# The up projection of a gated MLP: seven products of halves replaced by eight plain products

## The chip, the cores and the metric

The kernel runs on one core of a Trainium2 chip. The metric is the device time of one execution in microseconds (us). Engines are named as the profile names them: PE is TensorE (PEld its weight loads), DVE is VectorE, ACT is ScalarE, POOL is GpSimd, and SP is SyncE, whose queue issues nearly all DMAs here.

## The reference

Two layers of a block for a latent generator: a token mixer (a chunked state-space scan in both directions beside a diagonal recurrence) and a feed-forward part, for 1024 latent tokens and 256 context tokens of 1024 channels. The change concerns the feed-forward part only:

```python
def conv_ffn(h, w_up, conv_w, conv_b, w_down, rows):
    up = h @ w_up                                  # (tokens, 1024) x (1024, 2 * 2816)
    ...
    up = dwconv_centred(up, conv_w, conv_b)        # width 3 along tokens, within a grid row of 64
    gate, val = jnp.split(up, 2, axis=-1)
    return (jax.nn.silu(gate) * val) @ w_down      # (tokens, 2816) x (2816, 1024)
```

Layer 0 computes it for all 1280 tokens, layer 1 (the last) for the 1024 latent tokens alone. All data are float32.

## The kernel before

Activations lie with channels on the 128 partitions and tokens along the free dimension. A float32 operand is used as two parts, a rounded one (`hi`) and the remainder (`lo`), and each product is the sum of three matmuls, hi x hi, hi x lo and lo x hi (`mm3`, L746). Making the parts of an operand takes a cast on ACT and a subtraction on DVE or POOL (`split_act`, L977, for activations; `split_to`, L876, for weights).

The feed-forward part goes over the tokens in two blocks, called passes here: 640 tokens each in layer 0, 512 each in layer 1. In a pass (`ffn_halves`, L1492) the 2816 hidden channels are 22 tiles j, in 8 groups of 2 or 3. For the tiles of a group (and the first of the next one) `up(j)` computes 128 gate and 128 value channels into the two rows `fr0` and `fr1`; then `gate` applies the convolution (ACT L1511, DVE L1518 and L1520), SiLU and the product, and splits the result (`g`). Then the down products of the group are added to eight accumulators (`acc`, DVE L1597), with down weights that are loaded (`raw`, L1555) and split (`wd`, L880, L881) on the way. PSUM has four banks for these products (`psm`, tile `mm`).

The up products are done by a scheme of seven products instead of eight. The weights of tile j are four blocks (gate or value, first or second half of the 1024 input channels), the activations four blocks (first or second half of the input channels, first or second half of the block's tokens). `halves` (L844) makes the seven combinations of the activations, `lefts` (L884) those of the weights: three sums and one difference on POOL, seven splits by ACT with DVE (four) or POOL (three). Each of the seven operands is stored to DRAM (`kept`, L926), 512 KB each, and in the second pass it is loaded from there in place of the raw weights (L945). `seven` (L949) multiplies each with one half of the tokens, 4 x 3 matmuls of 320 columns (layer 0) or 256 (layer 1), and adds the results into `fr0` and `fr1` by DVE out of PSUM (L958).

The operands wait in a ring of slots (`ws`; 5 in layer 0, 7 in layer 1). `W.fill` fills it ahead of a tile, and after each product `W.step` makes the next one; the raw weights (`rw`) have 4 or 6 buffers. All instructions of an engine run in the order in which they are written; SP's loads and stores too. Between the products, `self.tick()` lets background work go on: the modulation vectors (`adaw`, only in layer 0's passes) and the streamed residual and norm of the other block (`stream`, L1621, tiles `xs`, `xk`), which load and store through SP's queue. `tail` makes the activations of the second pass during the last group's down products of the first.

## Time and profile before

| what | value |
|---|---|
| median of 3 runs | 3623.93 us (3618.96 to 3641.98) |
| profiled execution, its own time | 3592.94 us |
| its span, first to last instruction | 3591.1 us |
| mean granted clock of TensorE, share of full speed | 0.915 |
| PE busy | 3036.1 us, 85% |
| DVE busy | 2510.9 us, 70% |
| ACT busy | 1363.1 us, 38% |
| POOL busy | 1070.4 us, 30% |
| read from and written to DRAM | 471.33 MB, 271.09 MB |

The shares are means over the whole span, which has phases with different limits; the feed-forward passes run from 893 to 2011 us (layer 0) and from 2717 to 3577 us (layer 1). A busy PE counts from a matmul's start to its modelled end, so that neighbours overlap; the distance between starts tells what a matmul costs.

### The profile page before, as it was taken

Reading aid. Unit: us, or ns where it says so; the run is one execution under the profiler, and the core shown is the slowest. Engines: PE = TensorE matmul, PEld = TensorE weight load, DVE = VectorE, ACT = ScalarE, POOL = GpSimd, SP = SyncE. Lnnn points to the kernel's source line nnn. Section 1 sums busy time; section 2 is a strip of 40 time slices with the busy share of each in tenths; the row PEclk is TensorE's granted clock in tenths of the full one; section 3 lists DMA queues with packets and bytes.
Section 4 is the critical chain, followed back from the end, with each engine's and each line's share of the span. In section 5 each row is a group of like instructions: output and inputs, shape, how many; then the busy total and the mean of one; then the engine's idle time right before and its main releaser. Section 6 shows DMA issues by size and latency. Waiting matters only on the chain.

```text
span 3591.1 us, 53144 instructions
## 1 busy us (share of the span) xinstructions
PE 3036.1 (85%) x19123; PEld 2687.2 (75%) x19123; DVE 2510.9 (70%) x4661; ACT 1363.1 (38%) x2422; POOL 1070.4 (30%) x819
## 2 busy tenths in 40 slices
PE   7689869898688989889999789748887688889998
PEld 4578657687568989868899788746676677778997
DVE  5867963557757787855465897973578788876666
ACT  4324514545333333432122444514445444433223
POOL 3642441233324454200000332441245355510000
PEclk9899988898799999999999899878898899999999
DMA  7354587333886666787666445467256787768774
GB/s 244 107 159 149 156 242 218 114 108 112 273 289 215 222 233 217 262 307 247 230 226 215 132 122 168 129 186 200 91 161 218 271 282 264 270 251 295 265 281 180
DMA packets 583083, 745.94 MB, mean 208 GB/s; under 512 B 66116, under 2 KB 423118, under 8 KB 582821
## 3 DMA queue, kind: packets, MB, share of 16 engines
q1 hardware_dynamic: 582341, 742.38, 62.5%
q8 instruction: 152, 2.49, 0.3%
q14 instruction: 110, 0.90, 0.1%
q0 software_dynamic: 480, 0.17, 0.1%
HBM read 471.33 MB, written 271.09 MB: 207 GB/s over the span
## 4 chain that ended last, share of the span: by engine, by line
PE 37%; DVE 21%; DMA 6%; issue 4%; ACT 3%; SPq 1%; POOL 1%; DVEq 0%; ACTq 0%; POOLq 0%
PE mm L751 11%; PE mm L753 10%; PE mm L752 10%; PE ps L55 5%; DVE fc L1518 2%; DVE fc L1520 2%; DVE fr L958 2%; DVE ws L881 1%; DMA adaw<-in_w_ada_dram 1%; DVE X L550 1%; DVE sc L545 1%; ACT fc L1511 1%; DVE X L517 1%; DVE acc L1597 1%; DMA up<-ws 1%
## 5 line engine op out<-in xcount | busy, mean ns | idle before, releaser
L751 PE MATMUL mm<-unit,ws 128*128 128x320 f32 (+1 forms) x2464 | 749.2, 304 | 75.5 <-DVE fr L958 43.3
L753 PE MATMUL mm<-unit,ws 128*128 128x320 f32 (+1 forms) x2464 | 742.0, 301 | 6.5 <-DVE ws L881 4.3
L752 PE MATMUL mm<-unit,ws 128*128 128x320 f32 (+1 forms) x2464 | 742.6, 301 | 1.7 <-POOL unit L860 1.2
L751 PEld LDWEIGHTS mm<-unit,ws 128*128 128x128 f32 x2464 | 477.1, 194 | 103.7 <-DVE fr L958 49.1
L753 PEld LDWEIGHTS mm<-unit,ws 128*128 128x128 f32 x2464 | 477.7, 194 | 10.9 <-DVE ws L881 6.3
L752 PEld LDWEIGHTS mm<-unit,ws 128*128 128x128 f32 x2464 | 478.2, 194 | 6.5 <-issue 3.4
L958 DVE TENSOR_TENSOR fr<-mm,fr 128x320 f32<-128x320 f32 (+1 forms) x616 | 270.3, 451 | 277.7 <-PE mm L753 275.3
L751 PE MATMUL mm<-unit,whi 128*128 128x320 f32 (+3 forms) x1264 | 425.7, 338 | 38.3 <-ACT unit L979 23.4
L753 PE MATMUL mm<-unit,wlo 128*128 128x320 f32 (+3 forms) x1264 | 416.3, 330 | 9.7 <-POOL wlo L742 9.5
L752 PE MATMUL mm<-unit,whi 128*128 128x320 f32 (+3 forms) x1264 | 417.9, 331 | 7.0 <-POOL unit L980 5.6
L742 POOL TENSOR_TENSOR wlo<-raw,whi 128x1024 fp32r<-128x1024 f32 (+1 forms) x86 | 201.4, 2342 | 365.0 <-ACT whi L741 343.6
L751 PE MATMUL mm<-g,wd 128*128 128x320 f32 (+3 forms) x708 | 254.7, 361 | 60.5 <-ACT wd L880 36.2
L751 PEld LDWEIGHTS mm<-unit,whi 128*128 128x128 f32 x1264 | 250.4, 199 | 73.5 <-ACT unit L979 26.3
L1511 ACT ACTIVATE fc<-fr,fcols 128x640 f32<-128x640 f32 (+1 forms) x176 | 144.1, 862 | 350.4 <-DVE fr L958 350.2
L753 PE MATMUL mm<-g,wd 128*128 128x320 f32 (+3 forms) x708 | 249.6, 357 | 25.7 <-DVE wd L881 25.5
L1597 DVE TENSOR_TENSOR acc<-mm,acc 128x320 f32<-128x320 f32 (+3 forms) x336 | 183.2, 552 | 123.2 <-PE mm L753 122.4
L753 PEld LDWEIGHTS mm<-unit,wlo 128*128 128x128 f32 x1264 | 250.0, 198 | 24.9 <-POOL wlo L742 13.9
L752 PEld LDWEIGHTS mm<-unit,whi 128*128 128x128 f32 x1264 | 250.7, 198 | 19.7 <-POOL unit L980 6.5
L752 PE MATMUL mm<-g,wd 128*128 128x320 f32 (+3 forms) x708 | 251.4, 355 | 1.1 <-DVE g L1530 1.1
L1518 DVE SCALAR_TENSOR_TENSOR fc<-fr,fcols,fc 128x255 f32<-128x255 f32 (+2 forms) x220 | 190.5, 894 | 58.7 <-ACT fc L1511 57.5
L751 PEld LDWEIGHTS mm<-g,wd 128*128 128x128 f32 x708 | 142.0, 201 | 89.1 <-ACT wd L880 44.3
L881 POOL TENSOR_TENSOR ws<-rw,ws 128x512 fp32r<-128x512 f32 x88 | 133.2, 1515 | 219.4 <-ACT ws L880 214.6
(412 smaller groups left out, 6519.6 us busy)
## 6 DMA issues: line engine op xcount, KB each, us to landing
up<-ws SPq DMA_DIRECT2D x308, 512.0 KB
ws<-up SPq DMA_DIRECT2D x308, 512.0 KB
rw<-in_ffn_w_up_dram SPq DMA_DIRECT2D x176, 256.0 KB
adaw<-in_w_ada_dram SPq DMA_DIRECT2D x80, 512.0 KB
raw<-in_ffn_w_down_dram SPq DMA_DIRECT2D x96, 384.0 KB
raw<-in_w_in_dram SPq DMA_DIRECT2D x40, 512.0 KB
raw<-in_w_out_dram SPq DMA_DIRECT2D x32, 512.0 KB
unit<-in_w_ada_dram SPq DMA_DIRECT2D x32, 256.0 KB
```

Of the source, the lines that this page charges most:

```text
L55: i = f(*a, **k)
L517: v.scalar_tensor_tensor(o, col(g, a, k, nj), T["lam"][:, 0, i, g:g + 1], o, op0=OP.mult, op1=OP.add)
L742: (eng or nc.vector).tensor_tensor(lo[:, :m], raw[:, :m], hi[:, :m].bitcast(F32), op=OP.subtract)
L751: mm(ps, whi[:, k], ahi[:, sl], start=first and k == 0, stop=False)
L752: mm(ps, whi[:, k], alo[:, sl], start=False, stop=False)
L753: i = mm(ps, wlo[:, k], ahi[:, sl], start=False, stop=last and k == len(a) - 1)
L881: eng.tensor_tensor(lo, x, hi.bitcast(F32), op=OP.subtract)
L958: add = lambda o, ps, x: v.tensor_tensor(o, ps, x, op=OP.add)
L1511: nc.scalar.activation(c, r[s], AF.Identity, bias=f[3][:, ft:ft + 1], scale=f[1][:, ft:ft + 1])
L1518: v.scalar_tensor_tensor(cr[:, :, 1:], rr[:, :, :w - 1], f[0][:, ft:ft + 1], cr[:, :, 1:], op0=OP.mult, op1=OP.add)
L1520: v.scalar_tensor_tensor(cr[:, :, :w - 1], rr[:, :, 1:], f[2][:, ft:ft + 1], cr[:, :, :w - 1], op0=OP.mult, op1=OP.add)
L1597: v.tensor_tensor(acc[m][:, o:o + c], ps, acc[m][:, o:o + c], op=OP.add)
```

## The change

The up projection is computed as plain products. `splits` (in place of `halves`) splits each of the eight activation tiles, DVE and POOL in turn. `lefts` loads the raw weights of tile j in four pieces of 128 x 512, gate before value, splits each (ACT with POOL), stores nothing, and is given the list of all tiles twice, so that the second pass loads and splits the weights again. `ups` (in place of `seven`) multiplies a piece with all tokens of the block: four channel tiles x 3 matmuls for each piece of tokens (256 and 384, or 320 twice, in layer 0; 512 in layer 1). The first half of the channels opens the sum in PSUM and the second half closes it, and ACT copies the sum to `fr0` or `fr1`. A tile has four steps in place of seven; the gate of the tile before is advanced twice per step and background work after every second.

```diff
-    def halves(self, src, n, out, pool):
...
+    def splits(self, src, n, out, pool):
+        for k in range(KT):
+            out.append(self.split_act(src(k), n, self.nc.gpsimd if k % 2 else self.nc.vector))
             yield
...
-    def lefts(self, srcs, out, pool, kept):
...
+    def lefts(self, srcs, out, pool):
+        nc, g = self.nc, self.nc.gpsimd
+        todo = [(p, i) for p in srcs for i in range(2)]
+        raws = []
         def load():
             if todo:
                 p, i = todo.pop(0)
...
+                x = pool.tile([P, 4, P], F32, name="rw", bufs=self.nrw)
+                self.sp.last = nc.sync.dma_start(x, p[:, 4 * i:4 * i + 4])
+                raws.append(x)
+        for _ in range(3):
+            load()
         yield
...
+        while raws:
+            w = self.slot(pool)
+            out.append(self.split_to((w[:, 0], w[:, 1]), raws.pop(0), g))
+            load()
+            yield
+
+    def ups(self, W, b, n, pieces, r):
+        for t in r:
+            ps = [self.psm.tile([P, 512], F32, name="mm")[:, :c] for _, c in pieces]
+            for h in range(2):
+                w = W.take()
+                for (o, c), x in zip(pieces, ps):
+                    self.mm3(x, w, b[4 * h:4 * h + 4], slice(o, o + c), h == 0, h == 1)
+                if h:
+                    for (o, c), x in zip(pieces, ps):
+                        self.nc.scalar.copy(t[:, o:o + c], x)
                 yield
-    def seven(self, W, b, n, ra, rb):
...
-            for i, _ in enumerate(self.seven(W, B, n, *r)):
+            for i, _ in enumerate(self.ups(W, B, n, pieces, r)):
+                next(post, None)
                 next(post, None)
                 W.step()
-                if i in (2, 5):
+                if i % 2:
                     self.tick()
...
-        kept = [self.dram.tile([P, 7, 2, 4 * P], F32, name=f"up{l}{j}") for j in range(nt)]
-        LW = Stream(self.lefts([up(j) for j in range(nt)], ops, pw, kept), ops)
+        LW = Stream(self.lefts([x for _ in range(2) for j in range(nt) for x in up(j)], ops, pw), ops)
```

The calls of `halves` and `ffn_halves` become calls of `splits` and `ffn`, and `Stream.fill` stops when the generator is at its end.

## Rows read from the trace of the kernel before

**Rows 1.** Four passes: length, busy PE, PEld, DVE, ACT, POOL, clock, DMA share, GB/s.

```profile
893.00:1491.00 598.00, 498.07 (x3000) 460.52 (x2999) 451.72 (x731) 229.27 (x392) 247.23 (x175) 0.92 0.68 238
1491.00:2011.00 520.00, 489.92 (x3127) 449.94 (x3125) 306.60 (x622) 143.74 (x241) 26.85 (x23) 0.97 0.72 244
2717.00:3199.00 482.00, 382.95 (x2378) 340.24 (x2378) 390.66 (x566) 206.16 (x373) 229.88 (x156) 0.90 0.76 265
3199.00:3577.00 378.00, 364.90 (x2497) 333.49 (x2498) 246.43 (x490) 120.12 (x215) 2.02 (x2) 0.99 0.73 261
```

**Rows 2.** Timeline of TensorE, start and duration in us: 320, 256 and 512 columns.

```profile
1299.92 0.31 PE L751 MATMUL mm<-unit,ws 128*128 128x320 f32 x1
...
1303.89 0.31 PE L751 MATMUL mm<-unit,ws 128*128 128x320 f32 x1
...
3319.94 0.28 PE L751 MATMUL mm<-unit,ws 128*128 128x256 f32 x1
...
3322.76 0.28 PE L751 MATMUL mm<-unit,ws 128*128 128x256 f32 x1
...
3345.06 0.39 PE L751 MATMUL mm<-g,unit 128*128 128x512 f32 x1
...
3346.45 0.40 PE L751 MATMUL mm<-g,wd 128*128 128x512 f32 x1
```

**Rows 3.** Sums over up-product stretches: layer 0 first, second pass; layer 1 first, second.

```profile
sum 359.70, PE 309.96 PEld 290.94 DVE 273.35 ACT 150.07 POOL 167.13; mean PE 38.74 PEld 36.37 DVE 34.17 ACT 18.76 POOL 20.89
...
sum 308.50, PE 296.66 PEld 279.31 DVE 163.39 ACT 72.49 POOL 0.48; mean PE 37.08 PEld 34.91 DVE 20.42 ACT 9.06 POOL 0.06
...
sum 277.70, PE 241.68 PEld 236.58 DVE 236.81 ACT 127.88 POOL 156.59; mean PE 30.21 PEld 29.57 DVE 29.60 ACT 15.98 POOL 19.57
...
sum 222.80, PE 220.95 PEld 219.74 DVE 131.03 ACT 53.64 POOL 0.00; mean PE 27.62 PEld 27.47 DVE 16.38 ACT 6.71 POOL 0.00
```

**Rows 4.** Sums over down-product stretches, the same four passes in the same order.

```profile
sum 237.20, PE 185.57 PEld 168.31 DVE 179.78 ACT 81.34 POOL 81.73; mean PE 23.20 PEld 21.04 DVE 22.47 ACT 10.17 POOL 10.22
...
sum 203.60, PE 186.86 PEld 167.03 DVE 138.84 ACT 69.70 POOL 24.26; mean PE 23.36 PEld 20.88 DVE 17.35 ACT 8.71 POOL 3.03
...
sum 205.90, PE 142.50 PEld 104.68 DVE 155.44 ACT 80.13 POOL 74.35; mean PE 17.81 PEld 13.08 DVE 19.43 ACT 10.02 POOL 9.29
...
sum 141.90, PE 132.38 PEld 103.94 DVE 104.02 ACT 60.55 POOL 0.00; mean PE 16.55 PEld 12.99 DVE 13.00 ACT 7.57 POOL 0.00
```

**Rows 5.** Waits of TensorE, us, times, longest: layer 1 first, layer 0 second pass.

```profile
PE mm L751 <- ACT wd L880: 33.0, 6, 14.5
PE mm L751 <- DVE fr L958: 25.1, 17, 2.8
PE mm L753 <- DVE wd L881: 17.9, 9, 3.7
...
PE mm L751 <- ACT unit L859: 3.5, 1, 3.5
...
PE mm L751 <- DMA ws<-up: 8.1, 3, 3.6
```

**Rows 6.** Groups of GpSimd and ScalarE, first pass of layer 1: splitting an up weight.

```profile
L881 POOL TENSOR_TENSOR ws<-rw,ws 128x512 fp32r<-128x512 f32 x42 | 62.6, 1491 | 69.4 <-ACT ws L880 66.6 <-issue 2.8
...
L880 ACT CAST ws<-rw 128x512 fp32r<-128x512 f32 x84 | 50.6, 616 | 17.3 <-PE mm L753 13.0 <-POOL rw L923 2.8 <-DMA rw<-in_ffn_w_up_dram 1.1
```

**Rows 7.** Waits of SP's queue, first pass of layer 1.

```profile
SPq L55 <- POOL ws L881: 40.9, 24, 5.9
```

**Rows 8.** Groups of VectorE in layer 1: first pass, then (last row) second pass.

```profile
L958 DVE TENSOR_TENSOR fr<-mm,fr 128x256 f32<-128x256 f32 x154 | 61.9, 413 | 14.8 <-PE mm L753 14.1
L1518 DVE SCALAR_TENSOR_TENSOR fc<-fr,fcols,fc 128x504 f32<-128x504 f32 x44 | 54.7, 1262 | 16.7 <-ACT fc L1511 16.7
...
L1518 DVE SCALAR_TENSOR_TENSOR fc<-fr,fcols,fc 128x504 f32<-128x504 f32 x44 | 32.0, 743 | 20.3 <-ACT fc L1511 20.3
```

**Rows 9.** Busy time in one down stretch, second pass of layer 1.

```profile
3341.60:3358.40 16.80, 16.80 (x74) 13.52 (x74) 12.21 (x21) 6.27 (x12) 0.00 (x0) 1.00 0.46 166
```

More of the change, by code (lines that the diff above doesn't have):

```diff
@@ L88, in step @@
     def step(self):
-        next(self.gen, None)
+        return next(self.gen, self) is not self
     def fill(self, n):
-        while len(self.out) < n:
-            self.step()
+        while len(self.out) < n and self.step():
+            pass
     def take(self):
@@ L882, in split_to @@
         return hi, lo
-    def lefts(self, srcs, out, pool, kept):
-        nc, v, g = self.nc, self.nc.vector, self.nc.gpsimd
-        m = 4 * P
-        todo = [(p, i) for p in srcs for i in (2, 3, 0, 1)]
-        spots = iter([(d, i) for d in kept for i in range(7)])
-        late = []
-        def store():
-            w, (d, i) = late.pop(0)
-            self.sp.dma_start(d[:, i], w)
-        def put(x, eng):
-            w = self.slot(pool)
-            out.append(self.split_to((w[:, 0], w[:, 1]), x.rearrange("p (k n) -> p k n", n=P), eng))
-            late.append((w.bitcast(F32), next(spots)))
-            if len(late) > 2:
-                store()
+    def lefts(self, srcs, out, pool):
+        nc, g = self.nc, self.nc.gpsimd
+        todo = [(p, i) for p in srcs for i in range(2)]
+        raws = []
         def load():
@@ L940, in lefts @@
-        while late:
-            store()
-        for d in kept:
-            for i in range(7):
-                w = self.slot(pool)
-                self.sp.last = nc.sync.dma_start(w.bitcast(F32), d[:, i])
-                out.append([w[:, j].rearrange("p (k n) -> p k n", n=P) for j in range(2)])
-                yield
-    def seven(self, W, b, n, ra, rb):
-        v = self.nc.vector
-        lo, hi = slice(0, n // 2), slice(n // 2, n)
-        def mul(i):
-            ps = self.psm.tile([P, 512], F32, name="mm")[:, :n // 2]
-            self.mm3(ps, W.take(), b[i], slice(0, n // 2))
-            return ps
-        add = lambda o, ps, x: v.tensor_tensor(o, ps, x, op=OP.add)
-        self.nc.scalar.copy(ra[:, lo], mul(0))
-        yield
-        add(ra[:, hi], mul(1), ra[:, lo])
-        yield
-        add(rb[:, hi], mul(2), ra[:, hi])
-        yield
-        add(rb[:, lo], mul(3), rb[:, hi])
-        yield
-        ps = mul(4)
-        add(rb[:, hi], ps, rb[:, hi])
-        add(ra[:, hi], ps, ra[:, hi])
-        yield
-        add(ra[:, lo], mul(5), ra[:, lo])
-        yield
-        add(ra[:, hi], mul(6), ra[:, hi])
-        yield
+                x = pool.tile([P, 4, P], F32, name="rw", bufs=self.nrw)
@@ L1489, in wout, with ffn @@
         self.free(*itertools.chain(*a))
-    def ffn_halves(self, l, blk, B, W, new, pr, pool, pw, ng, before, tail, done):
+    def ffn(self, l, blk, B, W, new, pr, pool, pw, ng, before, tail, done):
         nc, v = self.nc, self.nc.vector
@@ L1570, in ffn_halves @@
             if gi + 1 == ng:
-                self.free(*itertools.chain(*itertools.chain(*B)))
+                self.free(*itertools.chain(*B))
                 for _ in post:
@@ L1618, in chain @@
         self.free(R)
-        yield from self.halves(lambda k: self.normed(mt, k, blk, S, A, B, pool), blk[1], out, pool)
+        yield from self.splits(lambda k: self.normed(mt, k, blk, S, A, B, pool), blk[1], out, pool)
     def stream(self, blk, md, R, G, A, B, hd, pool):
@@ L2054, in finish @@
             yield from self.prenorm(acc, blk, R[1], self.prs[1]["A1"], self.prs[1]["ada"], H[1], pn)
-        tail = self.halves(load(0), n1, H2[1], pn)
-        self.ffn_halves(l, blks[0], H2[0], LW, new, pr, pg, pw, 8, before, tail, away(md[1]))
+        tail = self.splits(load(0), n1, H2[1], pn)
+        self.ffn(l, blks[0], H2[0], LW, new, pr, pg, pw, 8, before, tail, away(md[1]))
         if last:
@@ L2063, in layer @@
             tail, done = first_next(), squares
-        acc = self.ffn_halves(l, blks[1], H2[1], LW, new, pr, pg, pw, 8, before, tail, done)
+        acc = self.ffn(l, blks[1], H2[1], LW, new, pr, pg, pw, 8, before, tail, done)
         if not last:
```

50 lines of the change are left out of this document (removed).

## The prediction

> **What bounds the kernel now.** I read the page's shares first, then the busy time of each engine in the four passes of the feed-forward part (two blocks of tokens in each of two layers), because the change touches nothing else. These passes last 598, 520, 482 and 378 us [rows 1], 1978 of the 3591 us span. The reader should compare the two passes of one layer: they do the same products, and yet the first is 78 us longer than the second in layer 0 and 104 us longer in layer 1. In the second passes TensorE is busy nearly throughout at a granted clock of 0.97 and 0.99 (the upper level, 2.4 GHz, but for a few moments); in the first it is busy 83% and 79% of the time, at 0.92 and 0.90, which mixes in stretches at the lower level after waits. The first passes differ in one thing: there the weights are loaded, combined by GpSimd, split into two parts and stored; in the second passes the stored operands are loaded. VectorE is busy 451.72 and 390.66 us in the first passes against 306.60 and 246.43 in the second, GpSimd about 230 to 250 against 27 and 2 [rows 1]. So second passes are bound by TensorE and first passes by what prepares operands.
>
> Next I asked what one product costs when nothing stops TensorE: the distance between starts. 27 starts of 320 columns are 3.97 us apart, 147 ns each; 24 of 256 columns are 2.82 us apart, 117.5 ns each; 6 of 512 columns are 1.39 us apart, 232 ns each [rows 2]. That is 0.45 to 0.46 ns a column at every width: **columns are what is paid**, and wider products are not cheaper per column.
>
> Last I cut each pass into stretches of up products and of down products. Up: 359.70 us in the first pass of layer 0, 308.50 in the second; layer 1: 277.70 and 222.80 [rows 3]. Down: 237.20 and 203.60; 205.90 and 141.90 [rows 4]. The extra time of the first passes lies in both.
>
> **The change part by part.**
>
> *More columns.* Seven products of 4 x 3 matmuls on half the tokens become eight on half the tokens, or the same columns in wider pieces. Per tile j and pass in layer 0: 84 x 147 ns = 12.35 us becomes, at 96 matmuls of 320 columns, 14.11 us (block 0 has pieces of 256 and 384 columns, the same sum of columns). In layer 1: 84 x 117.5 ns = 9.87 us becomes 48 x 232 ns = 11.14 us. With 22 tiles in each of two passes that is 44 x 1.76 = 77.5 and 44 x 1.27 = 56 us: **+133.5 us**, all on the engine that sets the end wherever it doesn't wait.
>
> *The up stretches of the first passes.* Out go the four GpSimd sums per tile, three of seven splits, every store, and all VectorE additions out of PSUM, whose results TensorE had to wait for (25.1 us in the first pass of layer 1 [rows 5]); and a slot no longer has to be stored before it is used again. In their place come four splits on GpSimd per tile, at 1491 ns [rows 6] 6.0 us, beside 14.1 or 11.1 us of products. A weight now serves one and a half to two times as much TensorE work in a step, so the five or seven slots hold twice the lead. The result stays in PSUM over two steps and is copied by ScalarE. ScalarE is busy 206.16 of 482 us in the fullest of these passes [rows 1], and at 616 ns a cast [rows 6] it loses 66 casts per first pass; if that cover were gone, each copy would cost about a cast's 0.6 us, 176 copies in layer 0 and 88 in layer 1, some 160 us. Its new copies wait for the end of a sum; behind them on ScalarE stand the gate's steps and the cast of the next slot, for which VectorE, GpSimd and, four to six steps later, TensorE wait: 14 us or more of lead against a copy. On SP a load of raw weights now waits for a GpSimd split two to four steps back, and the down weights' loads queue behind it, but no longer behind seven stores per tile. I take the up stretches of the first passes down to the level of the second ones. The second passes' rows leave out 12 and 24 products that run between the last down products of the pass before (12 x 0.147 = 1.8 and 24 x 0.1175 = 2.8 us): 359.70 - 308.50 - 1.8 = 49.4, and 277.70 - 222.80 - 2.8 = 52.1, together **-101.5 us**.
>
> *The down stretches of the first passes.* They aren't edited. TensorE waits there for down weights whose loads stand behind the stores on SP's queue (SP waited 40.9 us for GpSimd's splits before a store [rows 7]; TensorE waited 33.0 us for casts of down weights), and for VectorE's split of them, 17.9 us [rows 5]. With the stores and half of VectorE's backlog gone, at best the second pass's level is reached: 33.6 + 64.0 = 97.6 us. At worst nothing, because SP still issues the streamed residual there and waits for its pieces, also new waits for the raw weights' buffer. I take three quarters, **-73 us**: the row of SP's waits names the splits, which go.
>
> *The second passes.* Operands are no longer loaded (TensorE waited 8.1 us for them [rows 5]): **-8 us**. But GpSimd now makes 88 splits in each, where it had almost nothing to do, and ScalarE 88 casts (54 us at 616 ns [rows 6], into a ScalarE that is idle two thirds of these passes [rows 1]). What GpSimd does to VectorE is seen in one shape: the convolution's step takes 743 ns in the second pass of layer 1 and 1262 ns in the first, beside GpSimd [rows 8]. VectorE loses its PSUM additions, 154 x 413 ns = 64 us by the first pass's row [rows 8]. What it gains in stretched steps: at least nothing, at most the whole of each GpSimd step, 88 x 1.491 = 131 us [rows 6]; the row gives 0.52 us for each of 88 convolution steps, 46 us, with half as many other steps of the gate some 69 us, scaled by 88 GpSimd steps for the 154 of before some 40 us. As 40 is under 64, I take nothing for TensorE.
>
> The Trainium skill, "SBUF — State Buffer", section "SBUF: two separate sides", speaks against the change at this point: GpSimd and VectorE share one pair of SBUF ports as an exclusive lock, held for a whole instruction, which touches VectorE's instructions with two SBUF inputs. The rows agree: the convolution's steps stretch from 743 to 1262 ns. By that rule, at its worst, every split would hold a VectorE instruction for its whole length; the time that this gives is that of rival (c).
>
> *Loads.* The up weights are read again in the second passes (88 loads of 256 KB more) and 308 stores and 308 loads of 512 KB go; the DMA engines are busy 0.68 to 0.76 in these passes [rows 1], so transfers gain room. Nothing taken. The split of the activations replaces the combinations of halves between passes: the wait before the first product of layer 1 (3.5 us [rows 5]) goes, **-3.5 us**; at worst it stays.
>
> *Sum.* 133.5 - 101.5 - 73 - 8 - 3.5 = -52.5 us. The profiled execution took 3592.94 us by its own time, 1.8 us more than its span, and would become 3540. The median of the runs, 3623.93, is 31 us higher; I take the difference as it is: 3623.9 - 52.5 = **3571 us**.
>
> **The rivals.** (a) The down stretches keep all their waits: they come from the order on SP's queue and the streamed residual, which stay. For it: the longest wait of TensorE there, 14.5 us [rows 5], is for a load. Against: the stores before it go. 133.5 - 101.5 - 8 - 3.5 = +20.5 us, 3644 us.
> (b) Full recovery: the down stretches reach the second pass's level: -77 us, 3547. This is the fast end of the forecast's own case; beyond it, the second passes' down stretches still hold 203.6 - 1056 x 0.147 = 48 and 141.9 - 528 x 0.232 = 19 us over their products [rows 2, 4], of which a third might go (-22 us).
> (c) Slower: VectorE becomes the bound in the down stretches of the second passes, because GpSimd's splits stretch its steps. Place: a stretch of three tiles in layer 1 holds 12.21 us of VectorE's work in 16.80 us [rows 9]. It decides from the point at which more than 4.6 us is added to such a stretch, 37 us over the eight of a pass. The 40 us above are at that point, if all fell into the down stretches; but most splits run beside the up products, where VectorE has the freed 64 us. If it lands, 35 to 40 us a pass on TensorE's path in both second passes, and the first passes keep their down waits: 20.5 + 75 = +95 us, 3719 us.
>
> **How the numbers follow.** The forecast with (b) as its fast end 0.64, (a) 0.20, (c) 0.12, others 0.04 (half of them slower). About 1%, 36 us, is what a measurement of this kernel can tell from no change. In the forecast's case the time lies from -100 to -10 us, 0.58 of it beyond -36. (a) lies within 1%, with a little of it above +36 us. So faster 0.60, same 0.25, slower 0.15. The range leaves out (c) and the last tenth of the fast end: from 3623.9 - 77 - 22 - 10 (the unknown of the loads and of the median) = 3515 to a little over (a), 3650 us.
>
> **What would show it.** Right: the four passes' lengths near 562, 551, 406 and 406 us (598 + 38.8 - 49.4 - 25, 520 + 38.8 - 8, 482 + 28 - 52.1 - 48 - 3.5, 378 + 28); in the first passes TensorE's granted clock at 0.96 or above and VectorE's busy time near that of the second passes; no waits for PSUM additions in the up stretches; up stretches of three tiles in 42 us (layer 0) and 34 us (layer 1); the distance of starts unchanged at 232 ns for 512 columns. Wrong: waits for down weights of 30 us or more in the first pass of layer 1 as now (rival a); convolution steps above 1100 ns in the second passes together with TensorE's waits for VectorE's split of down weights (rival c); or starts of 512 columns further apart when they follow each other for 11 us.

## The result, and the profile of the changed kernel

The changed kernel takes **3461.75 us** (median of 4 runs, 3450.99 to 3467.04), the kernel before 3622.12 us (median of 4 runs, 3618.96 to 3641.98): a ratio of 0.956, 95% interval 0.952 to 0.960. It is 160 us faster where 52.5 were forecast, and lies below the range of 3515 to 3650 us. The sign was right, the size was not.

The profiled execution took 3467.04 us (span 3465.3 us, mean granted clock 0.934). First the busy time of the four passes, as in [rows 1], cut here from the first up product of a layer to the end of the last down product of a pass; then the sums over the stretches of the two first passes, as in [rows 3, 4]: up and down of layer 0, up and down of layer 1.

```profile
894.40:1412.00 517.60, 498.09 (x3286) 475.91 (x3285) 262.00 (x470) 217.61 (x388) 147.79 (x110) 0.99 0.38 119
1412.00:1945.70 533.70, 519.02 (x3384) 480.74 (x3384) 261.91 (x463) 215.19 (x390) 139.52 (x106) 0.99 0.42 130
2663.10:3057.50 394.40, 379.80 (x1617) 302.68 (x1616) 237.25 (x316) 187.38 (x331) 128.77 (x95) 0.98 0.41 126
3057.50:3450.90 393.40, 384.28 (x1683) 308.98 (x1683) 229.30 (x320) 177.36 (x313) 113.12 (x83) 0.99 0.34 103
...
sum 336.30, PE 329.60 PEld 317.28 DVE 145.67 ACT 153.26 POOL 112.56; mean PE 41.20 PEld 39.66 DVE 18.21 ACT 19.16 POOL 14.07
...
sum 182.00, PE 169.19 PEld 161.00 DVE 116.04 ACT 63.81 POOL 34.53; mean PE 21.15 PEld 20.13 DVE 14.51 ACT 7.98 POOL 4.32
...
sum 251.40, PE 250.30 PEld 202.81 DVE 138.57 ACT 121.82 POOL 108.09; mean PE 31.29 PEld 25.35 DVE 17.32 ACT 15.23 POOL 13.51
...
sum 145.50, PE 132.00 PEld 102.14 DVE 99.83 ACT 66.59 POOL 21.18; mean PE 16.50 PEld 12.77 DVE 12.48 ACT 8.32 POOL 2.65
```

The reader should see that the difference between a first and a second pass is gone: 394.4 and 393.4 us in layer 1. In layer 0 the first pass is even 16 us shorter; it holds 64 modulation products of 512 columns against 128 in the second (an estimate: 64 x 0.232 = 15 us). TensorE is busy 96 to 98% of each pass at a granted clock of 0.98 or 0.99, VectorE about the same time in both passes of a layer, and the share of the DMA engines has fallen from 0.7 to 0.4.

TensorE's waits, us, times, longest, in the first pass of layer 0, then of layer 1, where [rows 5] had 33.0, 25.1 and 17.9 us:

```profile
PE ps L55 <- DMA adaw<-in_w_ada_dram: 8.9, 8, 4.2
PE mm L751 <- ACT g L1449: 2.9, 1, 2.9
PE ps L55 <- DVE rs L251: 2.2, 2, 1.1
...
PE mm L751 <- ACT wd L859: 5.1, 2, 4.9
PE mm L753 <- DVE wd L860: 2.7, 3, 1.6
```

SP's own wait for GpSimd's splits, the row on which the forecast leant [rows 7], is five times as long in the same pass of layer 1 and does no harm, for TensorE has no wait for an up weight (`ws`) in either first pass:

```profile
SPq L874 <- POOL ws L860: 217.6, 88, 5.6
```

The distance between starts is unchanged, 24 of 512 columns in 5.56 us, 232 ns each (timeline, first and last):

```profile
2912.78 0.40 PE L753 MATMUL mm<-unit,ws 128*128 128x512 f32 x1
...
2918.34 0.39 PE L753 MATMUL mm<-unit,ws 128*128 128x512 f32 x1
```

**Where the 160 us lie.** With before's passes cut in the same way (table below), they fall from 1983.9 to 1839.1 us: -144.8. (In [rows 1] they are cut at 1491 and 3199, but the first passes end at 1494.2 and 3210.1: by the cut used here a first pass was 91 and 130 us longer than the second, not 78 and 104.) Outside them the changed kernel loses 19: 6 before the first pass, 13 between the layers. There TensorE has one wait that the kernel before does not have, in the token mixer, which the change does not touch. It stands behind one subtraction on GpSimd that took 31.78 us; the next one of the same shape took 2.37:

```profile
PE mm L753 <- POOL ub L996: 19.0, 1, 19.0
...
2026.08 31.78 POOL L742 TENSOR_TENSOR wlo<-raw,whi 128x1024 fp32r<-128x1024 f32 x1 [18.92 <-ACT whi L741]
2057.81 0.11 POOL L996 MEMSET ub<- 128x16 f32 x1
2057.87 2.37 POOL L742 TENSOR_TENSOR wlo<-raw,whi 128x1024 fp32r<-128x1024 f32 x1
```

So the profiled executions are 125.9 us apart. The other 34.5 are between profile and median: before's profiled execution (3592.94) is 29 us faster than its median, after's 5 us slower than its own.

Lengths of the passes in us, and in brackets TensorE's time in up and in down products (from the start of each product to the start of the next), for the kernels below:

| kernel | layer 0, first | second | layer 1, first | second |
|---|---|---|---|---|
| before | 605.6 (361 / 245) | 514.7 (311 / 203) | 497.0 (285 / 212) | 366.6 (223 / 144) |
| after | 517.8 (337 / 180) | 533.5 (339 / 194) | 394.6 (250 / 144) | 393.2 (252 / 141) |
| e1 no stores | 596.2 (357 / 239) | 512.7 | 466.5 (290 / 177) | 367.5 |
| e2 no sums | 577.8 (333 / 245) | 517.8 | 432.1 (242 / 190) | 367.5 |
| e3 no additions | 608.9 (353 / 256) | 514.2 | 486.0 (271 / 215) | 364.3 |
| e4 made anew | 598.5 | 551.4 | 474.5 | 447.6 |
| e5 neither | 521.4 (314 / 207) | 512.8 | 403.3 (241 / 163) | 368.2 |
| e6 plain, kept | 524.8 | 526.6 | 391.2 | 389.0 |
| e7 plain, sums | 620.0 (346 / 274) | 604.1 (358 / 246) | 460.0 (257 / 204) | 444.7 (251 / 193) |
| e8 copies on VectorE | 511.0 | 529.9 | 388.0 | 393.2 |
| e9 other queue | 620.3 (400 / 221) | 519.8 | 487.9 (300 / 188) | 368.7 |
| e10 e7, other queue | 622.0 (344 / 278) | 614.3 | 436.1 (260 / 176) | 412.0 (253 / 158) |
| e11 splits on VectorE | 503.6 | 531.1 | 379.2 | 385.8 |
| e12 e8, other queue | 513.6 | 533.8 | 397.2 | 392.7 |
| e13 seven, a third | 568.4 (301 / 268) | 455.0 | 466.1 (198 / 269) | 340.2 |
| e14 plain, a third | 411.8 | 394.3 | 316.7 | 303.8 |
| e15 all on VectorE | 499.4 | 527.1 | 380.5 | 384.0 |
| e16 splits in turn | 511.4 | 530.9 | 387.0 | 390.2 |

### The profile page after: what moved, and what is told of

Read it like the earlier page. It is cut to its first block, busy times and chain, and to the rows that moved or that the text cites. A ratio compares the mean times of both kernels' runs of the same rounds, so it can differ in the third digit from the quotient of the medians.

```text
span 3465.3 us, 48617 instructions
## 1 busy us (share of the span) xinstructions
PE 3088.8 (89%) x18067; PEld 2673.7 (77%) x18067; DVE 2060.4 (59%) x3789; ACT 1454.7 (42%) x2610; POOL 1104.2 (32%) x847
## 5 line engine op out<-in xcount | busy, mean ns | idle before, releaser
L860 POOL TENSOR_TENSOR ws<-rw,ws 128x512 fp32r<-128x512 f32 x352 | 483.9, 1377 | 1033.4 <-ACT ws L859 764.0
L752 PE MATMUL mm<-unit,ws 128*128 128x320 f32 (+3 forms) x2112 | 714.8, 338 | 3.4 <-POOL unit L901 3.4
L751 PE MATMUL mm<-unit,ws 128*128 128x320 f32 (+3 forms) x2112 | 716.5, 339 | 0.2 <-ACT unit L900 0.2
L753 PE MATMUL mm<-unit,ws 128*128 128x320 f32 (+3 forms) x2112 | 713.5, 338 | 0.0
L1439 DVE SCALAR_TENSOR_TENSOR fc<-fr,fcols,fc 128x255 f32<-128x255 f32 (+2 forms) x220 | 207.3, 958 | 492.7 <-ACT fc L1432 492.7
L751 PEld LDWEIGHTS mm<-unit,ws 128*128 128x128 f32 x2112 | 398.0, 188 | 46.6 <-issue 10.1
L752 PEld LDWEIGHTS mm<-unit,ws 128*128 128x128 f32 x2112 | 398.0, 188 | 36.1 <-POOL unit L901 4.6
L753 PEld LDWEIGHTS mm<-unit,ws 128*128 128x128 f32 x2112 | 397.9, 188 | 34.7 <-issue 3.4
L742 POOL TENSOR_TENSOR wlo<-raw,whi 128x1024 fp32r<-128x1024 f32 (+1 forms) x86 | 230.6, 2682 | 361.9 <-ACT whi L741 328.2
L859 ACT CAST ws<-rw 128x512 fp32r<-128x512 f32 x352 | 218.4, 621 | 206.0 <-PE mm L753 116.8
L1519 DVE TENSOR_TENSOR acc<-mm,acc 128x256 f32<-128x256 f32 (+2 forms) x336 | 185.0, 554 | 171.2 <-PE mm L753 170.3
L751 PE MATMUL mm<-g,wd 128*128 128x320 f32 (+3 forms) x708 | 243.7, 345 | 10.8 <-ACT wd L859 6.8
L753 PE MATMUL mm<-g,wd 128*128 128x320 f32 (+3 forms) x708 | 241.5, 343 | 6.5 <-DVE wd L860 6.3
L752 PE MATMUL mm<-g,wd 128*128 128x320 f32 (+3 forms) x708 | 242.0, 342 | 0.0
L895 ACT COPY fr<-mm 128x320 f32<-128x320 f32 (+3 forms) x264 | 125.2, 476 | 195.1 <-PE mm L753 194.8
L1441 DVE SCALAR_TENSOR_TENSOR fc<-fr,fcols,fc 128x255 f32<-128x255 f32 (+2 forms) x220 | 176.0, 815 | 3.5
## 6 DMA issues: line engine op xcount, KB each, us to landing
raw<-in_ffn_w_down_dram SPq DMA_DIRECT2D x96, 384.0 KB
```

Source lines behind the costliest of these rows:

```text
L742: (eng or nc.vector).tensor_tensor(lo[:, :m], raw[:, :m], hi[:, :m].bitcast(F32), op=OP.subtract)
L751: mm(ps, whi[:, k], ahi[:, sl], start=first and k == 0, stop=False)
L752: mm(ps, whi[:, k], alo[:, sl], start=False, stop=False)
L753: i = mm(ps, wlo[:, k], ahi[:, sl], start=False, stop=last and k == len(a) - 1)
L859: self.nc.scalar.copy(hi, x)
L860: eng.tensor_tensor(lo, x, hi.bitcast(F32), op=OP.subtract)
```

## The experiments

All ratios are to runs of the kernel before on the same chip, with 95% intervals; differences in us are worked out from ratios, at 3620 us for the kernel before. The first six take the change apart.

**e1: seven products, no stores.**

```diff
+            spot = next(spots)
+            if spot[0] is kept[0]:
+                late.append((w.bitcast(F32), spot))
...
-        for d in kept:
+        for _ in kept:
+            d = kept[0]
```

> The seven products, but only the first tile's seven operands are stored; the second passes load those same seven for every tile, with the same sizes and number of loads, so their products use the wrong weights. Theory S (the first passes of the kernel before wait because 154 stores of 512 KB per layer stand on SP's queue ahead of the down weights and hold the slots): the down stretches of the first passes fall from 237 and 206 us to below 210 and 155 us, the time by 90 to 140 us. Theory V (they wait because VectorE and GpSimd are behind with sums, splits and additions, whose steps hold each other up): no more than 30 us go, and the waits for VectorE's split of down weights and for additions stay.

Measured: 3565.91 us, 0.988 (0.986 to 0.990), -45 us; neither expectation. The stores did what the forecast said of the down stretches in layer 1 (212 to 177 us; the wait for casts of down weights 33.0 to 3.8 us) and next to nothing in layer 0. And other waits grew. TensorE in the first pass of layer 1, where [rows 5] had 25.1 for VectorE's additions:

```profile
PE mm L751 <- DVE fr L959: 35.6, 27, 3.7
PE mm L752 <- DVE g L1531: 10.7, 8, 2.0
```

**e2: seven products, no GpSimd sums.**

```diff
-            g.tensor_tensor(s1, a21, a22, op=OP.add)
...
-            g.tensor_tensor(s2, s1, a11, op=OP.subtract)
-            put(s2, v)
+            put(a21, v)
```

> The seven products with GpSimd's four sums per tile left out (raw blocks are split and stored in their place, so the sums of the weights are missing from the computation). Theory S: GpSimd's freed time brings the stores forward a little, 0 to 30 us. Theory V: GpSimd falls from 230 to 250 to about 110 us in the first passes, the convolution's step from 1262 towards 950 ns, and 60 to 120 us go.

Measured: 3511.41 us, 0.973 (0.970 to 0.975), -100 us, within what theory V expected. The up stretches of the first passes fall by 28 and 43 us; the down stretches of layer 1 lose 22, those of layer 0 keep all of theirs (245). In layer 1 the convolution's step falls from 1262 to 843 ns too. How much of the gain comes from a shorter chain of steps and how much from VectorE's shorter steps was not separated.

**e3: seven products, no additions by VectorE** (ScalarE copies in their place).

```diff
-        add = lambda o, ps, x: v.tensor_tensor(o, ps, x, op=OP.add)
+        add = lambda o, ps, x: self.nc.scalar.copy(o, ps)
```

> The seven products with each addition out of PSUM by VectorE replaced by a copy by ScalarE (the additions are left out of the computation). Theory S: 0 to 30 us, in the up stretches of the first passes alone. Theory V: VectorE loses 64 to 75 us in each pass, the first passes lose their waits for additions (19 and 25 us) and part of those for VectorE's splits, 50 to 90 us in all.

Measured: 3603.95 us, 0.996 (0.994 to 0.999), -14 us. The up stretches lose 9 and 14 us; the down stretches, not edited, gain 12 and 3. So VectorE's own load, from which this takes some 50 us in each first pass, is not by itself what sets these passes, although the copies that ScalarE makes instead are part of the result.

**e4: seven products, operands made anew in both passes.**

```diff
-        LW = Stream(self.lefts([up(j) for j in range(nt)], ops, pw, kept), ops)
+        LW = Stream(self.lefts([up(j) for _ in range(2) for j in range(nt)], ops, pw), ops)
```

> The seven products with the operands combined and split anew in each pass, nothing kept in DRAM. Theory S: the first passes gain as without stores, 90 to 140 us, the second passes take on GpSimd's work and lose 0 to 40 us: 60 to 130 us faster than before. Theory V: the first passes stay within 30 us, the second become as long as the first (78 and 104 us more): 100 to 180 us slower than before.

Measured: 3704.54 us, 1.028 (1.025 to 1.030), +99 us slower. The first passes, without stores, lose only 7 and 23 us; the second ones grow by 37 and 81 us, in layer 1 to nearly the length of the first. In this kernel the operands of seven products are not made as fast as TensorE uses them, with or without stores.

**e5: seven products, neither stores nor sums** (in the main e1 and e2 together).

> The seven products with both left out: the stores (but for the first tile's seven operands, which every tile of the second passes loads) and GpSimd's sums (raw blocks in their place), so the weights used are wrong. If stores and sums are two limits of which each takes over when the other goes (theory B), more goes than the 45 and 100 us of the two alone: 180 to 230 us faster than before, the first passes near 530 and 400 us. If the two are simply added up (theory A), 130 to 155 us.

Measured: 3428.32 us, 0.947 (0.944 to 0.950), -193 us, more than e1 and e2 together (-145). Only with both gone does the first pass of layer 0 come near the length of the second (521 and 513 us); that of layer 1 falls to 403, still 35 above its second. A link taken out alone is worth less than it is once the next one has gone.

**e6: plain products, operands kept in DRAM.**

```diff
+            late.append((w.bitcast(F32), next(spots)))
+            if len(late) > 2:
+                store()
...
+        kept = [self.dram.tile([P, 4, 2, 4 * P], F32, name=f"up{l}{j}") for j in range(nt)]
+        LW = Stream(self.lefts([x for j in range(nt) for x in up(j)], ops, pw, kept), ops)
```

> The plain products, but the four split operands of a tile are stored in the first pass and loaded in the second, as the kernel before did with its seven. Theory S (stores ahead of the down weights on SP's queue are a cost of their own): the first passes of layer 0 and 1 become 10 to 30 us longer each than in the kernel after (518 and 395 us), with waits for casts of down weights and for the modulation's loads back; the second passes lose GpSimd's splits and stay within 8 us. Together 15 to 60 us slower than the kernel after, still 100 to 145 us faster than before. Theory V (stores cost nothing where GpSimd and VectorE have room): within 10 us of the kernel after.

Measured: 3453.02 us, 0.954 (0.951 to 0.956), the time of the changed kernel. In layer 0 the first pass grows by 7 us and the second falls by 7; in layer 1 both fall by 3 and 4. With plain products stores and loads together cost nothing that shows in the whole, and splitting anew gains nothing: "no operands kept in DRAM" is worth nothing by itself.

**e7: the changed kernel, with one GpSimd sum per step whose result nobody reads.**

```diff
-            out.append(self.split_to((w[:, 0], w[:, 1]), raws.pop(0), g))
+            x, u = raws.pop(0), self.unit(4 * P)
+            out.append(self.split_to((w[:, 0], w[:, 1]), x, g))
+            g.tensor_tensor(u.rearrange("p (k n) -> p k n", n=P), x, x, op=OP.add)
+            self.free(u)
```

> The kernel after with one more GpSimd sum of 128 x 512 per step, four per tile in each pass, whose result nothing uses. GpSimd rises to some 240 us a pass, as in the first passes of the kernel before. If GpSimd's steps cost TensorE time by holding up VectorE on their own, 40 to 100 us slower than the kernel after; if they do so only together with the four splits and seven additions that VectorE no longer has (theory B), 0 to 25 us.

Measured: 3770.45 us, 1.041 (1.038 to 1.044): +308 us over the changed kernel, beyond every expectation. GpSimd is not full: its rows in the first pass of layer 0 show it idle for 222.6 us ahead of the sums (L883), nearly all for loads.

```profile
L860 POOL TENSOR_TENSOR ws<-rw,ws 128x512 fp32r<-128x512 f32 x89 | 126.9, 1427 | 121.6 <-ACT ws L859 121.6
L883 POOL TENSOR_TENSOR unit<-rw 128x512 f32<-128x512 f32 x90 | 97.2, 1080 | 222.6 <-DMA rw<-in_ffn_w_up_dram 219.0 <-DVE A L725 3.1 <-PE mm L753 0.5
```

The cause is a circle: the sum waits for a load, the load waits on SP for the split before it to free a buffer, and that split stands behind an earlier sum on GpSimd. (A sum is written behind the split of the same weights, but the trace mostly has the sums one or two weights ahead: the order on the engine is not the written one here.) The timeline shows one turn, in which the load is issued at 1098.28, when the split has ended, and the next sum starts at 1101.12. SP shows the period, six loads of up weights in 26.91 us and a load of down weights queued behind them:

```profile
1095.95 1.04 POOL L883 TENSOR_TENSOR unit<-rw 128x512 f32<-128x512 f32 x1 [3.02 <-DMA rw<-in_ffn_w_up_dram]
1096.95 1.30 POOL L860 TENSOR_TENSOR ws<-rw,ws 128x512 fp32r<-128x512 f32 x1
1101.12 1.04 POOL L883 TENSOR_TENSOR unit<-rw 128x512 f32<-128x512 f32 x1 [2.88 <-DMA rw<-in_ffn_w_up_dram]
...
1098.28 26.91 SPq L874 DMA_DIRECT2D rw<-in_ffn_w_up_dram  x6
1125.59 0.37 SPq L1480 DMA_DIRECT2D raw<-in_ffn_w_down_dram  x1
```

That is (26.91 - 0.37) / 5 = 5.3 us a step against 14.11 / 4 = 3.5 us of products. But the time is not lost where the circle is: up stretches grow by 9 and 6 us in the first passes, down stretches by 93 and 59, although the sums are issued with the up products.

**e8: the changed kernel, copies out of PSUM by VectorE.**

```diff
-                        self.nc.scalar.copy(t[:, o:o + c], x)
+                        self.nc.vector.tensor_copy(t[:, o:o + c], x)
```

> The kernel after with the copies out of PSUM on VectorE in place of ScalarE. VectorE gains 20 to 40 us a pass of 240 to 260. If TensorE's columns are the bound in all four passes, within 12 us of the kernel after; if VectorE's order was what the change relieved, 20 to 60 us slower.

Measured: 3432.40 us, 0.948 (0.945 to 0.951), 28 us faster than the changed kernel, which neither expectation had. Part of it is the 19 us wait in the mixer, which this kernel does not have; the four passes fall by 17 us together.

**e9: the kernel before, loads of down weights issued by ScalarE.**

```diff
-                self.sp.last = nc.sync.dma_start(raw, dap(self.I["ffn_w_down"], (l * self.dff + grp[0] * P) * D + m * P,
+                nc.scalar.dma_start(raw, dap(self.I["ffn_w_down"], (l * self.dff + grp[0] * P) * D + m * P,
```

> The kernel before with the loads of the down weights issued from ScalarE's queue in place of SP's, nothing else changed. Theory Q (the down stretches of the first passes wait because the down weights' loads stand on SP's queue behind stores and up weights' loads that wait for late splits): the down stretches of the first pass of layer 1 fall from 206 to 175 to 185 us, those of layer 0 from 237 to 215 to 230, the waits for casts of down weights from 33 to below 8 us, 35 to 70 us in all. Theory W (VectorE is late itself with splits and additions): within 12 us of before.

Measured: 3619.31 us, 1.002 (0.999 to 1.004): nothing. TensorE's waits in the first pass of layer 1: the one for down weights (ACT wd) goes from 33.0 us [rows 5] to 8.9, and casts of up weights (ACT ws) take its place.

```profile
PE mm L751 <- ACT ws L880: 19.5, 5, 7.6
PE mm L751 <- DVE fr L958: 18.8, 11, 3.3
PE mm L753 <- DVE wd L881: 10.2, 4, 5.7
PE mm L751 <- ACT wd L880: 8.9, 7, 2.2
```

Down stretches lose 24 us in each first pass, up stretches gain 38 and 15. So the order on SP's queue decided where TensorE waited, but not for how long: theory Q had the place about right and the gain wrong. That the waits in the down stretches were the lag of the up operands, handed on, fits this but is not shown by it alone, since the edit also puts 34 and 32 loads per first pass into ScalarE's order, ahead of its casts. What that costs without a lag is seen in e12 against e8, 3 and 9 us in the first passes.

**e10: e7 with the same change of queue.**

> The plain products with the unused GpSimd sum per step, and the down weights' loads on ScalarE's queue. Theory Q: the down stretches, 41 us for three tiles in layer 0 and 25.7 in layer 1 with the sums alone, fall to 22 to 28 and 17 to 20 us; 170 to 300 us faster than with the sums alone (3770 us). Theory W: the sums hold VectorE's split of down weights up all the same, less than 60 us are won back.

Measured: 3713.18 us, 1.027 (1.022 to 1.033), 50 us less than e7, in size what theory W expected. It comes from layer 1 (down stretches 204 to 176 and 193 to 158). Layer 0 stays, since TensorE waits there for down weights that GpSimd itself splits, behind its sums (30.0 us, four times).

**e11, e12 and e16: who makes what.** e11 is the changed kernel with the up weights split by VectorE; e16 uses GpSimd and VectorE in turn; e12 is e8 with the queue of e9.

```diff
-            out.append(self.split_to((w[:, 0], w[:, 1]), raws.pop(0), g))
+            out.append(self.split_to((w[:, 0], w[:, 1]), raws.pop(0), nc.vector))
```

> The kernel after with the splits of the up weights on VectorE in place of GpSimd. If GpSimd's steps, which stretch VectorE's, cost TensorE time in the kernel after (the third rival of the prediction, in part), 10 to 40 us faster than it; if TensorE's columns are the bound, within 12 us of it, though VectorE then does 88 splits of some 0.7 us more per pass (about 60 us, less the 27 to 48 us of stretching).

> The plain products with the copies out of PSUM on VectorE and the down weights' loads on ScalarE's queue: both to see whether more is to be had. Waits for down weights were already small with the plain products (5 us in the first pass of layer 1), so 0 to 15 us faster than with the copies on VectorE alone (ratio 0.948); if a wait of ScalarE for a free buffer holds up its other work, up to 20 us slower.

> The kernel after with GpSimd and VectorE splitting the up weights in turn. If every GpSimd step costs a little through VectorE's stretched steps, half the gain of VectorE alone: ratio 0.949 to 0.952; if the gain was only in GpSimd's order of work elsewhere, 0.945 or 0.956.

Measured: e11 3420.10 us, 0.945 (0.941 to 0.950), 38 us faster than the changed kernel; e12 3446.27 us, 0.953 (0.948 to 0.957), no gain over e8, in whose first passes TensorE's waits for casts of down weights are 0.2 us at most; e16 3446.77 us, 0.953 (0.950 to 0.956), 12 us faster, which the intervals do not tell from the changed kernel. The passes tell more: 1839.1 us together in the changed kernel, 1819.5 in e16, 1799.8 in e11, so half of the gain for half of the splits, which is what the first expectation for e16 was about.

**e13: the kernel before, with one of three matmuls in every up product.** TensorE loses 22 x 56 x 0.147 = 181 us a pass in layer 0 and 145 in layer 1; all else stays. If TensorE sets a pass's time, the pass falls by about that; if the preparing of operands does, it stays.

```diff
-            self.mm3(ps, W.take(), b[i], slice(0, n // 2))
+            self.mm1(ps, W.take(), b[i], slice(0, n // 2))
```

> The kernel before with one of three matmuls in each up product (rounded part by rounded part; the other two are left out). TensorE loses 181 us of work in each pass of layer 0, 145 us in each of layer 1. Theory R (the first passes go at the rate at which loads, sums, splits and stores follow each other over SP, GpSimd, VectorE and ScalarE, wherever TensorE comes to feel it): the first passes stay within 60 us of 600 and 490 us, the second lose 130 us or more each. Theory T (TensorE's own work still sets most of the first passes' length): all four passes fall alike, the first by 120 us or more each.

Measured: 3449.38 us, 0.954 (0.949 to 0.958). Busy time of the four passes:

```profile
903.50:1471.90 568.40, 383.87 (x1802) 324.64 (x1801) 455.91 (x740) 229.36 (x401) 247.51 (x176) 0.72 0.72 255
1471.90:1926.90 455.00, 352.71 (x1876) 285.87 (x1875) 303.07 (x614) 142.81 (x239) 24.87 (x21) 0.86 0.77 273
2632.00:3098.10 466.10, 296.57 (x1179) 234.29 (x1178) 383.92 (x581) 208.11 (x379) 235.26 (x158) 0.74 0.79 279
3098.10:3438.30 340.20, 285.23 (x1241) 229.14 (x1241) 240.28 (x479) 118.24 (x211) 1.28 (x1) 0.80 0.77 285
```

The first passes lose 37 and 31 us, a fifth of TensorE's saving, although TensorE stands idle for 185 and 170 us of them. Its granted clock also fell, from 0.92 and 0.90 to 0.72 and 0.74, so that its products took longer. By an estimate from the distances between starts (147, 117.5 and 232 ns at the upper level, the rest without a wait being slower products), of the 181 us some 83 came back as waits and 54 as slower products, of the 145 some 66 and 49. So 568 and 466 us is the most that the preparing takes there. No engine is full: VectorE, the fullest, is busy 456 of 568 us. GpSimd's waits in the first pass of layer 1 show one side of it: it waits for ScalarE, for VectorE and for a load in turn.

```profile
POOL ws L886 <- ACT ws L885: 82.5, 32, 6.2
POOL unit L938 <- DVE ws L886: 65.2, 10, 17.2
POOL unit L922 <- DMA rw<-in_ffn_w_up_dram: 28.9, 5, 12.7
```

The down stretches, without an edit, grow by 23 and 57 us: TensorE meets part of the lag there. The second passes fell by 60 and 26 us, less than half of what was expected: TensorE waits there 71.0 and 26.7 us for the loads of the stored operands, at DMA shares of 0.77 and granted clocks of 0.86 and 0.80, so they had less room than I gave them.

**e14: the changed kernel, the same third.**

> The same for the kernel after: TensorE loses 207 us in each pass of layer 0 and 163 us in each of layer 1. If preparing the weights has room beside the plain products (theory R, the other side), all four passes fall by 100 us or more each, to below 420 us in layer 0 and 300 us in layer 1; if the kernel after stands at the edge of the same rate, by less than 60 us each.

Measured: 3053.26 us, 0.844 (0.840 to 0.848).

```profile
890.00:1301.80 411.80, 326.01 (x1878) 290.48 (x1877) 299.29 (x472) 210.47 (x388) 156.72 (x110) 0.89 0.48 150
1301.80:1696.10 394.30, 338.37 (x1975) 292.52 (x1974) 293.45 (x461) 209.63 (x390) 160.13 (x105) 0.92 0.57 175
2417.00:2733.70 316.70, 246.75 (x915) 184.29 (x914) 248.80 (x318) 184.17 (x330) 143.47 (x95) 0.88 0.51 157
2733.70:3037.50 303.80, 245.90 (x980) 184.68 (x979) 237.57 (x321) 172.88 (x312) 126.24 (x83) 0.92 0.44 133
```

All four passes fall, by 78 to 139 us, the first ones by 106 and 78 where the kernel before gave 37 and 31. In layer 1 that is less than the 100 us expected, and the passes stay above 300 us. The preparing of the changed kernel needs at most 412 us in the first pass of layer 0, where the pass takes 518 with all products: there TensorE's columns are the bound.

**e15: the changed kernel, splits and copies both by VectorE** (e8 and e11).

> The plain products with both the splits of the up weights and the copies out of PSUM on VectorE. If the two gains (ratios 0.948 and 0.945 against 0.956) are of the same kind, one order of work in place of another, this comes out at 0.940 to 0.948; if VectorE, at some 300 us a pass, becomes late in layer 1, 0.95 to 0.97.

Measured: 3404.68 us, 0.941 (0.937 to 0.944), as expected for gains of the same kind: the fastest that computes the whole, 54 us below the changed kernel, though its interval meets e11's. Two passes, first and second of layer 1, and VectorE's convolution step in the second:

```profile
2624.90:3005.40 380.50, 375.66 (x1618) 301.11 (x1617) 276.23 (x449) 173.48 (x288) 6.42 (x5) 1.00 0.43 132
3005.40:3389.40 384.00, 380.46 (x1683) 306.95 (x1682) 266.84 (x445) 161.43 (x268) 1.31 (x1) 1.00 0.35 105
...
L1439 DVE SCALAR_TENSOR_TENSOR fc<-fr,fcols,fc 128x504 f32<-128x504 f32 x44 | 32.7, 743 | 13.6 <-ACT fc L1432 13.6
```

Without splits on GpSimd TensorE is busy 99% of these passes, at full clock.

## Why the prediction was wrong, point by point

The passes were to take 562, 551, 406 and 406 us; they take 518, 534, 395 and 393. The granted clock of the first passes is above the 0.96 named, VectorE's busy time is that of the second passes, and no up stretch waits for an addition: but for the lengths, what was to show the mechanism is there.

**The columns: right.** Forecast +38.8 and +28 us a pass. The up products of the second passes grew by 27.9 and 29.4 us (311.2 to 339.1, 222.7 to 252.1); of the 38.8 in layer 0 the wait for operand loads, 8.1 us in [rows 5], goes off. Up stretches of three tiles take 42.3 and 33.6 us, as forecast.

**The second passes: right in kind, 13 us too dear.** They grew by 18.8 and 26.6 us, 45.4 together, for 66.8 - 8 = 58.8. Their down stretches also fell, by 9.1 and 2.9 us: the waits that rival (b) held possible.

**The up stretches of the first passes: too small by 24 us.** Net of the columns the forecast was 38.8 - 49.4 = -10.6 and 28 - 52.1 = -24.1. Measured: -23.9 and -34.6. The step "I take the up stretches of the first passes down to the level of the second ones" used as a floor what was none: in layer 0 the second pass holds some 15 us more modulation products, and waits of its own for loads. Another 9 of the 24 us lay in pieces of the stretches that [rows 3] left out (359.70 and 277.70 of 361.1 and 285.0 us).

**The down stretches of the first passes: the step that failed.** "I take three quarters, -73 us: the row of SP's waits names the splits, which go." Measured: -64.1 and -67.8, **-131.9 us** (244.5 to 180.4, 212.1 to 144.3). The step costed each wait by its releaser and gave the down stretches a cause of their own, the order on SP's queue, part of which stays. The runs showed another one. The chain load, sum, split, store, over four engines, sets the rate of a first pass of the kernel before: 568 and 466 us even when TensorE has 181 and 145 us less to do (e13), part of which came back through its lower clock. TensorE meets that lag in up and down stretches alike. Change the queue, and time goes from the down into the up stretches and the whole stays (e9; ScalarE's own part in that is not separated). Put a circle of waits into the preparing of the changed kernel, and the time appears in the down stretches, 93 of 102 us in layer 0 (e7). Take out one link and less goes than with two (45 and 100 us alone, 193 together: e1, e2, e5); with two gone, the first passes give back 84 and 94 us of the 91 and 130 by which they were longer than the second ones. So there was no fixed share of waits to be kept: where the chain is faster than TensorE (e14: at most 412 us where the pass with all products takes 518), nearly all of them go.

Of the 58.9 us that were missing, 24.6 are the quarter that the forecast held back, 13.5 lay in pieces that [rows 4] left out (237.20 and 205.90 of 244.5 and 212.1 us), and the other 21 come from layer 0, where the second pass's level was no floor (180.4 us against 203.6; layer 1 stayed 2.4 above it).

By this account a first pass lies at TensorE's level, worked out here after the fact: in layer 0 the new second pass less 15 us (518.5; measured 517.8), in layer 1 that of the second pass (393.2; measured 394.6).

The clock has a part in it. By the same estimate as in e13, the 67.8 us of layer 1's down stretches are some 51 us of waits and 16 us of products that were slower before. [rows 7] shows, besides, only one of SP's waits. In the same view two longer ones are for VectorE, so the row named only a part of what held SP up:

```profile
SPq L55 <- DVE fr L958: 56.4, 44, 3.9
SPq L55 <- DVE ws L881: 41.3, 14, 9.8
```

**From the profile to the median.** "I take the difference as it is": 31 us. It was -5 after the change, so 34.5 us of the 160 come from here. It looks like chance and not like the change: the runs of the kernel before lie between 3596 and 3642 us in these comparisons, the profiled execution just below them at 3593. Why they spread so stays open.

**Outside the passes.** -3.5 us was forecast at the start of layer 1. The wait there fell to 1.1 us; but it lies inside the first up stretch, which [rows 3] hold as well, so that the forecast counted it twice. Outside, 19 us were lost. One 19.0 us wait behind a subtraction of 31.78 us on GpSimd explains most of it. In e15 the same subtraction takes 31.8 us and the wait is there, in e8 it takes 7.0 and the wait is not; why one instruction takes that long stays open.

Together, against a forecast of -52.5: -13.4 (second passes), -23.8 (up), -58.9 (down), -34.5 (median), and +3.5 + 19.0 outside make -108; -52.5 - 108 is the measured -160. (The forecast's 88 more loads are those of one layer; with both it is 176. Nothing was taken for them, so the sum does not change.)

**The rivals.** (a) fell: no wait for down weights above 5.1 us is left. (b) was the right direction and itself too small, as its floor was the second pass. (c) is there as a mechanism, not as a bound. The convolution's first step in the second pass of layer 1 went from 743 ns [rows 8] to 1070 and its second (L1441) to 1102, just above the 1100 that were to show the rival; but the waits for VectorE's split of down weights, which were to come with it, are 0.3 us there:

```profile
L1441 DVE SCALAR_TENSOR_TENSOR fc<-fr,fcols,fc 128x504 f32<-128x504 f32 x44 | 48.5, 1102 | 1.3
L1439 DVE SCALAR_TENSOR_TENSOR fc<-fr,fcols,fc 128x504 f32<-128x504 f32 x44 | 47.1, 1070 | 108.9 <-ACT fc L1432 108.9
...
PE mm L753 <- DVE wd L860: 0.3, 1, 0.3
...
L860 POOL TENSOR_TENSOR ws<-rw,ws 128x512 fp32r<-128x512 f32 x81 | 111.3, 1375 | 237.7 <-ACT ws L859 229.0 <-issue 8.6
```

VectorE is busy 229 of 393 us there, too far from full for the stretching to set the end. Taking the splits away from GpSimd brings the step back to 744 ns and gains 38 us in all (e11). Whether they come from VectorE's shorter steps or from splits that are done sooner was not separated.

## What to carry to other kernels

Where engines hand operands to one another in order, ask first which is slower over a whole pass, the preparing chain or the engine that uses its results, and measure it by taking work from the user (here a third of the matmuls left): if the pass stays, the chain sets it. Look at the granted clock in that run too, for it fell here (from 0.92 to 0.72) and took back part of the work saved. Where the chain sets the pass, a wait's releaser names the place where the lag surfaces, so waits are not to be costed one by one: in this kernel removing one link or changing a queue moved them, and nearly all went when the chain as a whole became the faster one. A GpSimd that has time to spare is not free to use beside VectorE: try both, on the chip.

## What the runs showed of the hardware that was not expected

GpSimd stretches VectorE's steps, and is itself stretched far less. VectorE's convolution step takes 742 to 743 ns with GpSimd idle, on average 1070 in a pass with GpSimd's splits and 1262 with its sums and splits [rows 8]; VectorE's additions out of PSUM stay at 686 to 688 ns in both kinds of kernel. A split takes 1375 ns on GpSimd on average, but 1291 also in the 7 of 81 cases in which no VectorE instruction runs beside it (second pass of layer 1 of the changed kernel), and 691 on VectorE with GpSimd idle (e15): most of that difference lies between the engines. Shortest, median and longest, for the split on GpSimd and the convolution's two steps:

```profile
L860 POOL TENSOR_TENSOR ws<-rw,ws x81: 1282/1298/1831, 3061.3 to 3407.1; 128x512 fp32r<-128x512 f32 x81
L1439 DVE SCALAR_TENSOR_TENSOR fc<-fr,fcols,fc x44: 730/1165/1203, 3068.5 to 3427.3; 128x504 f32<-128x504 f32 x44
L1441 DVE SCALAR_TENSOR_TENSOR fc<-fr,fcols,fc x44: 727/744/1878, 3069.3 to 3428.1; 128x504 f32<-128x504 f32 x44
```

The Trainium skill, "SBUF — State Buffer", section "SBUF: two separate sides", gives a reason, a port pair that VectorE's instructions with two SBUF inputs share with GpSimd and that the first to start holds for its whole instruction. The trace agrees: the steps with two SBUF inputs stretch, those out of PSUM do not. A single step came to 1878 ns, 743 and most of a split, but on average the step gained 327 ns, not the whole 1291.

TensorE's granted clock fell with its waits: in the first pass of layer 1 it is 0.90 before [rows 1], 0.74 with a third of the up products (e13, TensorE idle for 170 of 466 us), 0.98 after the change and 1.00 in e15, where it is idle for 5 of 380 us. Time at the lower level of 1.2 GHz is thus part of the 34.6 and 67.8 us that its stretches gave back, by the same estimate some 21 and 16 us; it was not measured by itself.
